# All projections of the second layer ahead of its attention: block products over 1024 tokens, results through DRAM

## The chip, the cores and the metric

The kernel runs on one core of one Trainium2 chip. TensorE (PE in the profile) multiplies matrices: it holds a 128x128 stationary operand and streams a moving operand of up to 512 columns past it into a bank of PSUM. VectorE (DVE), ScalarE (ACT) and GpSimd (POOL) do element-wise work; SyncE (SP) issues every DMA here, on one queue. The metric is device time of one execution in microseconds (us), as the median of several runs. Beside it there is one profiled execution with its own time and its span (first to last instruction).

## What is computed

A decoder trunk of two layers over 1024 tokens with model width 1024, all in 32-bit floating point.

```python
# layer 0: retention, 4 heads (query and key width 256, value width 512)
u = rms_norm(h, ret_norm_pre); q, k, v, g = split(u @ ret_w_in)
o = retention_chunkwise(rope(q), rope(k) / 16, v)
o = head_norm(o) * silu(g)
h = h + rms_norm(o @ ret_w_out, ret_norm_post)
# shared keys and values
k, v = split(rms_norm(h, kv_norm) @ w_kv)            # 8 heads: 128 and 256 wide
# layer 1: stick-breaking attention, 8 heads
q, g = split(rms_norm(h, sb_norm_pre) @ sb_w_in)
z = q @ k.T / sqrt(128)                              # strictly causal, s < t
A[t, s] = sigmoid(z[t, s]) * prod_{s < j < t} (1 - sigmoid(z[t, j]))
h = h + rms_norm((A @ v) * silu(g) @ sb_w_out, sb_norm_post)
```

Two norms act on the same residual stream after layer 0 (for keys and values, and for queries and gates), so both share one row of reciprocal root mean squares and differ only in their gains.

## The kernel before

**Numbers.** Every operand of a large product is split into a rounded high part and a remainder (`split`, lines 574 to 581: one ScalarE copy, one VectorE subtraction). A product is then three matmuls: high by high, high by low, low by high (`mm3`, lines 412 to 417). So a line of the profile that says L415, L416 or L417 is one of these three; the tile names tell which product it belongs to.

**Tiles.** The residual stream is held transposed, features on the partitions. The tokens go in two halves of 512. `xh` are the eight split tiles of a half's normalised stream, `whl` split weight tiles, `wraw` weights as loaded. PSUM has eight banks under four names: `ma`, `mb`, `z` and `o`, two each.

**Phases.** `run` (line 1521) walks through four phases: layer 0 for the first and second half ("A"), layer 1 for the first and second half ("C"). In a "C" phase there are four pairs of heads (`CPair`, line 1149). For each pair and half:

- `kqproj` (line 1155): keys and queries, features on the partitions, by `proj` (line 457): 8 k-tiles x 4 column blocks x 3 matmuls of 512 columns. The gain of the norm is multiplied into the weights when they are split (`gkq`, line 1142).
- `values` (line 1169): values with tokens on the partitions. Two pairs together form a matrix of 2 x 2 blocks (input features even and odd, token blocks of 256, 512 output columns each), multiplied with seven block products instead of eight (numbers 1 to 7). `vfirst` does five of the products with one pair, `vsecond` two with the next. The sums of the stream are written to DRAM (`T_d`, line 1098) and read again (`operand`, line 1219); the sums of weights for the second use too (`w_sums`, line 1107, to `S_d`).
- `gproj` (line 1305): gates by `proj` again, then the SiLU.
- `rows` (line 1319): for each head and block of 128 query tokens the scores (PSUM `z`), two sigmoids on ScalarE (lines 1337, 1338), the causal selection on GpSimd (lines 1342, 1343), a running product on VectorE (line 1345) and the product that gives the weights A (line 1346). The second half also meets the first half's keys, from DRAM (`k_d`).
- `mix` (line 1356): A is transposed on TensorE (line 1375), split to `AT`, and multiplied by the values into two `o` banks. `gate` (line 1396) multiplies by the gates and splits the result to `oT`.
- `out` (line 1316, `outproj` line 484): the output projection of a pair: its weights are loaded and split, the sum over the pairs is read from and written to DRAM for every block of 128 features (`y_d`). `finish` (line 1433) does the last pair in two half-width passes with the closing norm.

**Order.** `merge` (line 524) lays the steps of one piece beside those of another, for example a pair's scores beside its value products. The instructions written so are then put in order by a list scheduler, `arrange` (line 101): it knows each instruction's dependences, the number of buffers of every tile name (`BUFS`, line 319) and an estimated duration (`_time`, line 68), ranks instructions by how late they may run, and fixes one order for every engine's queue and for SP's. At run time each queue goes strictly in that order.

**Where the change sits.** The last output projection of layer 0's second half writes `y_d`; `a_post` (line 1008) reads it back, applies the closing norm, adds the input, writes the stream to `h_d`, and sums squares for the next norm. `c_prep` (line 1068) loads the stream of a half, multiplies it by the row and splits it.

Of the kernel before, what the change touches and what calls it, by code (L numbers as in the profile page):

```python
# [13 lines left out]
F32 = mybir.dt.float32  # L14
# [294 lines left out]
def trunk(ctx, tc, xT, wts, gains, trig, ident_in, cols, out):  # L309
# [174 lines left out]
    def outproj(base, oT, y_d, first, acc=None, tags=None):  # L484
# [4 lines left out]
        def sum_so_far(c):  # L489
            y = S("f2", [512])  # L490
            if not first:
                dma(y[:], y_d[c])
            return y
        sums = ahead(8, sum_so_far)

        def chunk(j):
# [21 lines left out]
            dma(y_d[c], y[:])  # L518
# [64 lines left out]
    def flat(x):  # L583
# [6 lines left out]
    k_d = [DRAM(f"k{h}", F32R) for h in range(8)]  # L590
    v_d = [[DRAM(f"v{p}{b}", F32R) for b in range(4)] for p in range(NPAIR)]
    T_d = [{n: [DRAM(f"T{t}{n}{i}", F32R) for i in range(2)] for n in (5, 6, 7, 4)} for t in range(2)]
    S_d = [{n: [dr.tile([128, 512], F32, tag=f"s{g}{n}{k}", name=f"s{g}{n}{k}") for k in range(4)]
            for n in (5, 6, 7, 3)} for g in range(2)]
# [131 lines left out]
    class AHead:  # L726
# [139 lines left out]
        def out(self, y_d, acc=None, tags=None):  # L866
            return outproj(self.base + 12, lambda: self.oT, y_d, self.h == 0, acc, tags)
# [140 lines left out]
    def a_post(t, y_d, acc):  # L1008
# [13 lines left out]
        def load(k):  # L1022
            y, raw = box[k] = pair(k) if t else (S("vo", [512]), S("vo", [512]))
            dma(y[:], y_d[k])
            dma(raw[:], xT[128 * k:128 * k + 128, HT * t:HT * t + HT])
# [36 lines left out]
    def pair(k):  # L1062

        x = S("S", [2, 512])
        return x[:, 0], x[:, 1]


    def c_prep(t):
        X = Ctx()
        X.xh = [None] * 8  # L1070
        raws = []

        def load(k):
            c2, c = divmod(k, 2)
            if c == 0:
                raw = S("S" if c2 < 2 else "A", [2, 512])
                raws.append(raw)
                dma(flat(raw), h_d[t][c2][:])
                V.tensor_tensor(raw[:], raw[:], rowh[0][:].unsqueeze(1).broadcast_to([128, 2, 512]), ALU.mult)
            x = X.xh[k] = hl("xh")  # L1080
            split((x[:, 0, :], x[:, 1, :]), raws[c2][:, c])

        def sums(kt):

            raw = raws[kt]
            for c in range(2):
                A_.activation(raw[:, c], raw[:, c], AF.Copy, scale=gcol(G_KV, 2 * kt + c))
            q = [raw[:, n // 2, 256 * (n % 2):256 * (n % 2) + 256] for n in range(4)]
            a, b = S("f2", [2, 256]), S("f2", [2, 256])
            V.tensor_tensor(a[:, 0], q[0], q[1], ALU.subtract)  # L1090
            V.tensor_tensor(a[:, 1], q[2], a[:, 0], ALU.subtract)
            V.tensor_tensor(b[:, 0], q[2], q[0], ALU.subtract)
            V.tensor_tensor(b[:, 1], q[3], a[:, 1], ALU.subtract)
            for f, ns in ((a, (5, 6)), (b, (7, 4))):
                x = S("AT", [2, 2, 256], F32R)
                split((x[:, :, 0, :], x[:, :, 1, :]), f[:])
                for j, n in enumerate(ns):
                    dma(T_d[t][n][kt // 2][:, 512 * (kt % 2):512 * (kt % 2) + 512], x[:, j].rearrange("p a b -> p (a b)"))

        X.sums = [lambda kt=kt: sums(kt) for kt in range(4)]  # L1100
        return X, [lambda k=k: load(k) for k in range(8)]

    def block(base, which, blk, kt):

        return wts[base + 4 + 16 * which + kt, :, 512 * blk:512 * blk + 512]

    def w_sums(g):

        base, box = 64 + 32 * g, {}

        def load(kt):
            if kt % 2:
                x = S("sc0", [2, 512])
                r = box[kt] = [x[:, 0], x[:, 1], S("tab", [512])[:], S("tab", [512])[:]]
            else:
                x, y = S("S", [2, 512]), S("S", [2, 512])
                r = box[kt] = [x[:, 0], x[:, 1], y[:, 0], y[:, 1]]
            for x, (which, blk) in zip(r, ((1, 0), (1, 1), (0, 0), (0, 1))):
                dma(x, block(base, which, blk, kt))

        def add(kt):
            b12, b22, b11, b21 = box[kt]
            V.tensor_tensor(b12, b12, b22, ALU.add)
            V.tensor_tensor(b11, b12, b11, ALU.subtract)
            V.tensor_tensor(b22, b22, b11, ALU.subtract)
            V.tensor_tensor(b21, b21, b11, ALU.subtract)
            for n, x in ((5, b12), (6, b11), (7, b22), (3, b21)):
                dma(S_d[g][n][kt][:], x)

        return in_turn(4, 1, load, add)  # L1130
# [11 lines left out]
    def gkq(kk):  # L1142
        return [(512 * c + 256 * s, 512 * c + 256 * s + 256, gcol((G_KV, G_SB)[s], 2 * kk + c))
                for c in range(2) for s in range(2)]

    def gone(which):
        return lambda kk: [(512 * c, 512 * c + 512, gcol(which, 2 * kk + c)) for c in range(2)]

    class CPair:
        def __init__(self, t, pr, X):  # L1150
# [535 lines left out]
```

## Time and profile before

| | |
|---|---|
| median of 3 runs | 1709.36 us (1708.68 to 1711.95) |
| profiled execution, its own time | 1709.47 us |
| its span | 1707.8 us |
| mean granted TensorE clock | 0.998 |
| matmuls | 8057 |
| busy: TensorE, VectorE, ScalarE, GpSimd | 1694.7, 1309.3, 888.2, 141.9 us |
| moved by DMA | 344.58 MB, 202 GB/s over the span |
| HBM read, written | 271.68 MB, 71.30 MB |

A group's row gives line, engine, operation, output tile, input tiles, shapes and count, then busy time and mean duration of one, then the idle time of that engine just before. TensorE's matmuls overlap one another, so their mean duration is more than the distance between two starts. The granted clock is a share of full speed.

### The profile page before, as it was taken

The numbers are of one execution on the slowest core, as the hardware profiler recorded it, in microseconds if no ns is written. First come the engines' busy times: TensorE is split into PE (matmuls) and PEld (weight loads), VectorE is DVE, ScalarE is ACT, GpSimd is POOL, SyncE is SP. The second block draws the span as 40 slices with busy tenths as digits, with TensorE's granted clock in tenths as the row PEclk, the third lists the DMA queues.
The fourth block names the chain that finished last, engine by engine and source line by source line (L and its number), as shares of the span: only waits on it lengthen the run. The fifth ranks groups of instructions, "written<-read, shape, count | busy, mean of one in ns | idle before, by whom it ended". The sixth has DMA issues, their size and how long they took to land.

```text
span 1707.8 us, 23993 instructions
## 1 busy us (share of the span) xinstructions
PE 1694.7 (99%) x8057; PEld 1414.8 (83%) x8057; DVE 1309.3 (77%) x2213; ACT 888.2 (52%) x1656; POOL 141.9 (8%) x275
## 2 busy tenths in 40 slices
PE   9999999999999999999999999999999999999997
PEld 7888888888888888888888888888888888888887
DVE  8766778799867988698878878667887756756865
ACT  6445546465545536355755544544665445545543
POOL 0000101010010000112010100000010001001001
PEclk9999999999999999999999999999999999999999
DMA  5226565667536676286886989667883763463523
GB/s 191 95 92 204 161 234 169 210 190 259 166 118 194 213 231 216 78 289 206 290 305 215 338 313 305 202 213 258 285 275 117 258 223 99 162 215 99 163 93 126
DMA packets 182250, 344.58 MB, mean 202 GB/s; under 512 B 20208, under 2 KB 24432, under 8 KB 182128
## 3 DMA queue, kind: packets, MB, share of 16 engines
q1 hardware_dynamic: 182128, 343.07, 60.9%
q8 instruction: 63, 1.03, 0.3%
q14 instruction: 59, 0.48, 0.1%
HBM read 271.68 MB, written 71.30 MB: 201 GB/s over the span
## 4 chain that ended last, share of the span: by engine, by line
PE 96%; DVE 2%; DMA 1%; issue 0%; ACT 0%; SPq 0%; POOL 0%; DVEq 0%
PE pmb L415 13%; PE pmb L417 12%; PE pmb L416 12%; PE pma L415 12%; PE pma L416 12%; PE pma L417 12%; PE po L417 5%; PE po L416 5%; PE po L415 5%; PE pz L1375 2%; PE pz L417 1%; PE pz L416 1%; PE pz L415 1%; PE pz L1003 1%; DMA ko<-in_xT_dram 0%; PE pz L551 0%
## 5 line engine op out<-in xcount | busy, mean ns | idle before, releaser
L577 ACT ACTIVATE whl<-wraw 128x512 fp32r<-128x512 f32 x322 | 190.3, 624 | 171.4 <-PE pmb L417 83.5
L578 DVE TENSOR_TENSOR whl<-wraw,whl 128x512 fp32r<-128x512 f32 x322 | 213.6, 686 | 65.8 <-ACT whl L577 64.8
L415 PE MATMUL pma<-xh,whl 128*128 128x512 f32 x384 | 153.1, 399 | 0.0
L415 PE MATMUL pmb<-xh,whl 128*128 128x512 f32 x384 | 152.5, 398 | 0.0
L417 PE MATMUL pma<-xh,whl 128*128 128x512 f32 x384 | 150.1, 391 | 0.0
L417 PE MATMUL pmb<-xh,whl 128*128 128x512 f32 x384 | 150.0, 391 | 0.0
L416 PE MATMUL pma<-xh,whl 128*128 128x512 f32 x384 | 149.9, 390 | 0.0
L416 PE MATMUL pmb<-xh,whl 128*128 128x512 f32 x384 | 149.7, 390 | 0.0
L580 ACT ACTIVATE whl<-wraw,gn 128x256 fp32r<-128x256 f32 (+1 forms) x146 | 82.0, 603 | 55.2 <-PE pmb L417 35.4
L1345 DVE TENSOR_TENSOR_SCAN sgn<-sgn 128x384 f32<-128x384 f32 (+4 forms) x64 | 86.6, 1355 | 28.0 <-POOL sgn L1343 27.9
L577 ACT ACTIVATE AT<-pz 128x512 fp32r<-128x512 f32 (+1 forms) x96 | 46.2, 486 | 108.3 <-PE pz L1375 106.3
L415 PE MATMUL pmb<-oT,whl 128*128 128x512 f32 x256 | 101.3, 396 | 0.0
L416 PE MATMUL pmb<-oT,whl 128*128 128x512 f32 x256 | 100.1, 391 | 0.0
L417 PE MATMUL pmb<-oT,whl 128*128 128x512 f32 x256 | 100.1, 391 | 0.0
L578 DVE TENSOR_TENSOR AT<-pz,AT 128x512 fp32r<-128x512 f32 (+1 forms) x96 | 52.9, 554 | 58.4 <-ACT AT L577 57.7
L1342 POOL TENSOR_SCALAR_AFFINE_SELECT A<-A 128x128 f32<-128x128 f32 x64 | 32.8, 513 | 770.5 <-ACT A L1337 770.5
L581 DVE SCALAR_TENSOR_TENSOR whl<-wraw,gn,whl 128x256 fp32r<-128x256 f32 (+1 forms) x146 | 83.8, 602 | 14.1 <-ACT whl L580 13.3
L577 ACT ACTIVATE whl<-S 128x512 fp32r<-128x512 f32 x104 | 63.4, 628 | 51.4 <-PE pmb L417 12.6
L417 PEld LDWEIGHTS pmb<-xh,whl 128*128 128x128 f32 x384 | 72.1, 188 | 15.8
L417 PEld LDWEIGHTS pma<-xh,whl 128*128 128x128 f32 x384 | 72.1, 188 | 15.6
L416 PEld LDWEIGHTS pmb<-xh,whl 128*128 128x128 f32 x384 | 72.3, 188 | 13.4
L415 PEld LDWEIGHTS pmb<-xh,whl 128*128 128x128 f32 x384 | 72.2, 188 | 13.4
(394 smaller groups left out, 4593.2 us busy)
## 6 DMA issues: line engine op xcount, KB each, us to landing
wraw<-in_wts_dram SPq DMA_DIRECT2D x521, 256.0 KB, 3.6
y<-f SPq DMA_DIRECT2D x120, 256.0 KB, 3.6
f<-y SPq DMA_DIRECT2D x88, 256.0 KB, 4.4
S<-in_wts_dram SPq DMA_DIRECT2D x44, 256.0 KB, 4.8
ko<-in_wts_dram SPq DMA_DIRECT2D x42, 256.0 KB, 4.6
vo<-in_wts_dram SPq DMA_DIRECT2D x41, 256.0 KB, 4.4
T<-AT SPq DMA_DIRECT2D x32, 256.0 KB, 4.8
sc<-T SPq DMA_DIRECT2D x16, 512.0 KB, 5.3
```

The source lines that it names most:

```text
L415: MM(p, lh, rh, start=start, stop=False, **kw)
L416: MM(p, lh, rl, start=False, stop=False, **kw)
L417: MM(p, ll, rh, start=False, stop=stop, **kw)
L577: A_.activation(dst[0], src, AF.Copy)
L578: V.tensor_tensor(dst[1], src, f32(dst[0]), ALU.subtract)
L580: A_.activation(dst[0], src, AF.Copy, scale=scale)
L581: V.scalar_tensor_tensor(dst[1], src, scale, f32(dst[0]), ALU.mult, ALU.subtract)
L1003: nc.tensor.transpose(pt[:, 128 * e:128 * e + 128], on[:, 128 * e:128 * e + 128], ident[:])
L1342: first = G.affine_select(a[:, dg], a[:, dg], [[-1, 128]], ALU.is_gt, 0.0, base=0, channel_multiplier=1)
L1345: V.tensor_tensor_scan(n[:, :W][:, ::-1], n[:, :W][:, ::-1], n[:, :W][:, ::-1], 1.0, ALU.mult, ALU.bypass)
L1375: nc.tensor.transpose(p[:, 128 * tb:128 * tb + 128], self.A[hh][tb][:, c0:c0 + 128], ident[:])
```

## The change

Layer 1 is written in a new order. All its projections, for all 1024 tokens, come first; their results go to DRAM; then sixteen heads (eight of each half) run one after the other, with the output projections beside them.

- **Keys, queries, gates** (`Feature`): the stream is a matrix of 2 x 2 blocks (features even and odd; first and second token half), and so are the weights of a pair (two column blocks of 256). Seven block products of 4 k-tiles, 2 output blocks of 128 and 512 tokens each take the place of the eight implicit in `proj`. Gains are multiplied into the loaded weights on ScalarE, sums of weights are made on VectorE, and the banks of PSUM go on accumulating from one product to the next where the scheme allows it.
- **Values** (`Values`): the seven products with blocks of 512 tokens, once for each group of two pairs.
- **The sums of the stream** are made once, in `w_turn`, between the two halves' streams, and stay in SBUF. Products 1 and 2 need the first half alone. Of three key and query pairs and one value group these two are computed before the turn ("early": product 1 goes to DRAM, `c_d`, and comes back later).
- **Output weights** are split once (`w_out`) beside the projections and stored split; `Att.out` loads them so. The running sum of the output projection stays in SBUF (`ys`).
- **Layer 0's last output projection** keeps its result in SBUF (`kept`), and `a_post` takes it from there.
- **The host** lays the weights of keys, queries and gates out by blocks (`_quads`).
- `T_d`, `S_d`, `c_prep`, `w_sums`, `CPair` and the rings of raw tiles go.

```diff
-    def outproj(base, oT, y_d, first, acc=None, tags=None):
+    def outproj(base, oT, y_d, first, acc=None, tags=None, kept=None):
...
-            dma(y_d[c], y[:])
+            if kept is None:
+                dma(y_d[c], y[:])
...
+    def w_turn(kept):
+        tags = {6: ["sgn", "sgn", "A", "ko"], 7: ["AT", "AT", "AT", "ko"], 4: ["v"] * 4}
+        B.x1, B.T = [None] * 4, {n: [None] * 4 for n in (5, 6, 7, 4)}
+        def make(kt):
+            q = [B.raws[kt][:, 0], kept[kt][:, 0], B.raws[kt][:, 1], kept[kt][:, 1]]
...
+            V.tensor_tensor(kept[kt][:], kept[kt][:], rowh[0][:].unsqueeze(1).broadcast_to([128, 2, 512]), ALU.mult)
+            B.x1[kt] = B.late[:, kt]
+            V.tensor_tensor(q[0], q[1], q[0], ALU.subtract)
+            V.tensor_tensor(q[1], q[3], q[1], ALU.subtract)
+            split((B.x1[kt][:, 0, :], B.x1[kt][:, 1, :]), q[3])
+            V.tensor_tensor(q[3], q[3], q[0], ALU.subtract)
+            V.tensor_tensor(q[2], q[2], q[3], ALU.subtract)
+            for n, r in ((5, q[0]), (6, q[3]), (7, q[1]), (4, q[2])):
+                x = B.T[n][kt] = B.far[:, kt] if n == 5 else hl(tags[n][kt])
+                split((x[:, 0, :], x[:, 1, :]), r)
...
+    class Feature:
...
+        def block(self, c, col):
...
+                    dma(raw, wts[self.base + 2 * c + col, :, 512 * i:512 * i + 512])
+                    for k in range(2):
+                        x = raw[:, 256 * k:256 * k + 256]
+                        A_.activation(x, x, AF.Copy, scale=gcol(self.gains[col], 2 * (2 * i + k) + c))
...
+        def chunk(self, n, e):
+            early, late = self.when == "early", self.when == "late"
+            over = {7: 6, 4: 6} if early else {6: 1, 7: 1, 4: 1}
...
+            p, w = self.bank[over.get(n, n)][e], self.w[n]
+            for kt in range(4):
+                x = B.x0[2 * kt + n - 1] if n < 3 else B.x1[kt] if n == 3 else B.T[n][kt]
+                at = slice(256 * kt + 128 * e, 256 * kt + 128 * e + 128)
+                mm3(p[:], w[:, 0, at], w[:, 1, at], x[:, 0, :], x[:, 1, :], fresh and kt == 0, kt == 3, goes_on=not fresh)
...
+    def put_kq(pr):
+        def put(t, col, e, src):
+            x = stage()
+            split((x[:, 0, :], x[:, 1, :]), src[:], QSCALE if col else None)
+            dma(kq_d[t][pr][2 * col + e][:], x[:, :, :].rearrange("p a b -> p (a b)"))
...
+    class Values:
...
+                for tb in tbs:
+                    tl = slice(128 * tb, 128 * tb + 128)
+                    mm3(banks[tb][:], x[:, 0, tl], x[:, 1, tl], w[:, 0, cl], w[:, 1, cl], fresh and kt == 0, kt == 3, goes_on=not fresh)
...
+    def w_out():
+        def one(pr, ng, i):
+            raw, x = raw_w(), stage()
+            dma(raw, wts[64 + 16 * pr + 12 + ng, :, 512 * i:512 * i + 512])
+            split((x[:, 0, :], x[:, 1, :]), raw)
+            dma(w_d[pr][ng][i][:], x[:, :, :].rearrange("p a b -> p (a b)"))
...
+    class Att:
...
+            tag = "xh" if hh else "A"
...
+                    for n in ("K", "Q"):
+                        box[n] = hl("xh")
+                        dma(flat(box[n]), kq_d[self.t][self.pr][hh + (2 if n == "Q" else 0)][:])
...
+                    g = S("sg", [512])
+                    dma(g[:], g_d[self.t][self.pr][j][:])
...
+        kq = [Feature(64 + 16 * p, (G_KV, G_SB), put_kq(p), "early" if p < 3 else "", c_d[p]) for p in range(NPAIR)]
...
+        full = (1, 2, 5, 6, 7, 3, 4)
+        order = [(x, n) for x in kq[:3] + [vs[0]] for n in (1, 2)]
+        opening = len(order)
+        order += [(x, n) for x in [vs[0]] + kq[:3] for n in (5, 6, 7, 3, 4)]
+        order += [(x, n) for x in kq[3:] + [vs[1]] + gs[:2] for n in full]
+        order += [(x, n) for x in gs[2:] for n in (1, 5, 6, 7, 4)]
+        ends = len(order)
+        order += [(x, n) for n in (2, 3) for x in gs[2:]]
...
+        for n in range(2, 16):
...
+            merge(A.mix(n % 2), (outs[8 * (n % 2):][:8], 0 if n % 2 else 1, 1), (rows_of(n + 1), 0, 1), (extra, 1, 1))
```

More of the change, by code (lines that the diff above doesn't have):

```diff
@@ L1100, in c_prep @@
[L1100 to L1130, printed above, removed]
+            x = B.x0[k] = hl("xh")
@@ L1420, in load @@
             c2, c = divmod(k, 2)
-            y, raw = box[k] = pair(k)
+            y, raw = box[k] = S("wraw", [512]), S("wraw", [512])
             dma(y[:], y_d[k])
@@ L1606, in run @@
[L1606 to L1616 removed]
+            else:
+                load = w_prep()
@@ L1618, in trunk @@
+        merge(first)
+        merge(second, (tail(0), 1, 1))
+        for s in tail(1):
+            s()
     run()
```

677 lines of the change are left out of this document (375 added, 302 removed).

## The prediction

> **What bounds the kernel now.** I read the page's busy times and chain of waits first, then the list of what TensorE waited for in the second layer, then stretches of that layer, then its groups and a few instructions in order of time. Columns of a stretch: its bounds and length, then busy time (count) of PE, PEld, DVE, ACT and POOL, the granted clock, the share of the DMA engines, GB/s.
>
> ```profile
> PE 1694.7 (99%) x8057; PEld 1414.8 (83%) x8057; DVE 1309.3 (77%) x2213; ACT 888.2 (52%) x1656; POOL 141.9 (8%) x275
> ...
> PE 96%; DVE 2%; DMA 1%; issue 0%; ACT 0%; SPq 0%; POOL 0%; DVEq 0%
> ```
>
> ```profile
> core 0 of [0], span 1707.8 us
> engine line waited for: us in total, times, longest us
> PE pz L1490 <- POOL col L1484: 1.0, 1, 1.0
> PE pz L1474 <- DVE acc L1467: 0.3, 1, 0.3
> PE pma L416 <- DVE qk L578: 0.2, 1, 0.2
> ```
>
> TensorE makes 96% of the chain. From 800 us on, where the second layer begins, it waited 1.5 us for others, 1.3 of that in the closing steps. So time is the sum of TensorE's steps, as long as the others keep up. How near they come:
>
> ```profile
> 750.00:775.00 25.00, 25.00 (x115) 20.71 (x114) 23.97 (x40) 17.00 (x32) 3.39 (x2) 1.00 0.86 281
> ...
> 950.00:1000.00 50.00, 50.00 (x241) 41.91 (x240) 35.71 (x62) 24.73 (x53) 6.97 (x13) 1.00 0.96 323
> ...
> sum 908.00, PE 898.20 PEld 754.41 DVE 668.44 ACT 470.92 POOL 70.14; mean PE 49.90 PEld 41.91 DVE 37.14 ACT 26.16 POOL 3.90
> ```
>
> VectorE was busy 23.97 of 25 us (96%) and DMA ran at 323 GB/s with TensorE still full. Neither is a bound until it passes those levels.
>
> **What is removed: matmuls.** A projection matmul streams 512 columns. The start-to-start step comes from a run of them without gaps (28 rows, first and last shown), the count from the groups between 800 us and the end:
>
> ```profile
> 1204.80 0.39 PE L416 MATMUL pmb<-qk,whl 128*128 128x512 f32 x1
> ...
> 1210.92 0.39 PE L416 MATMUL pma<-qk,whl 128*128 128x512 f32 x1
> ```
>
> ```profile
> L415 PE MATMUL pma<-xh,whl 128*128 128x512 f32 x256 | 102.3, 400 | 0.0
> L415 PE MATMUL pmb<-xh,whl 128*128 128x512 f32 x256 | 101.5, 397 | 0.0
> ...
> L415 PE MATMUL pmb<-qk,whl 128*128 128x512 f32 x32 | 12.4, 389 | 0.0
> ```
>
> (1210.92 - 1204.80)/27 = 0.2267 us a step; the 400 ns of the groups is a matmul's whole passage, of which the next hides nearly half. Keys, queries and gates are 2 x 256 x 3 = 1536 matmuls (three for each product of split numbers), as the loops say: 2 halves x 4 pairs x 2 kinds x 96. After the change, a pair and kind over 1024 tokens is 7 products x 2 column blocks x 4 k-tiles x 3 = 168 in place of 192, so 8 x 168 = 1344. The values have seven products already: 672 before and after. Scores, transposes, weighted sums and output projection keep their counts. So 192 steps go: 192 x 0.2267 = **43.5 us**. Against the profiled execution's 1709.47 us (span 1707.8, with 1.67 us around it; 0.11 above the median of the runs, 1709.36) that gives 1665.9 if nothing else changes.
>
> The Trainium skill (TensorE: Matmul & The Clock Gate, "Wait — 56ns, not 53.3ns?") has 215.7 ns as the warm step at 512 columns. By it 41.4 us would go and the sum would be 2.1 us higher. The row is 11 ns longer than the rule, and the sum goes by the row.
>
> **What is added before the attention.** The products for differences of the two token halves need the second half's normalised stream; only products 1 and 2 of three key/query pairs and of one value group can run before it: 3 x 2 x 24 + 2 x 48 = 240 matmuls, 54.4 us. In that time the first layer's closing norm must finish (eight adds with squares, two diagonals), and the turn forms all sums. VectorE's prices, from its groups between 760 and 1100 us (a 512-wide operation on two tiles is 0.69, with a scale 0.745):
>
> ```profile
> L581 DVE SCALAR_TENSOR_TENSOR whl<-wraw,gn,whl 128x512 fp32r<-128x512 f32 x21 | 15.6, 745 | 1.3 <-ACT whl L580 0.9
> L578 DVE TENSOR_TENSOR whl<-wraw,whl 128x512 fp32r<-128x512 f32 x23 | 15.4, 691 | 2.8 <-ACT whl L577 2.7
> ...
> L1030 DVE SCALAR_TENSOR_TENSOR S<-S,gn,acc 128x512 f32<-128x512 f32 x8 | 6.0, 748 | 6.5 <-ACT acc L571 3.6 <-DMA S<-y 2.9
> ...
> L1079 DVE TENSOR_TENSOR S<-S,acc 128x1024 f32<-128x1024 f32 x4 | 4.8, 1210 | 0.0
> ```
>
> - The norm: 8 scaled products 0.748, 8 sums and 7 squares' sums 0.69: 16.3; two diagonals of 8 narrow parts, each put at half of 0.69: 5.5.
> - The turn, four times: one 1024-wide product 1.21, four subtractions and five splits at 0.69: 4 x 7.4 = 29.7.
> - The three pairs' products 1 and 2: 12 weight splits, 6 sums, 6 output splits at 0.69: 16.6.
> - The value group, all seven products: 28 weight splits (16 scaled, 12 not), 16 scaled sums, 12 sums and 16 output splits: 32 x 0.745 + 40 x 0.69 = 51.4.
>
> Together 119 us of VectorE work for the 480 matmuls (108.8 us) up to the end of that value group. Some 6 us of it can lie outside (the first weights before, the last output splits after): 113 us. At 100% busy that is 4 us more than TensorE's work, at the best 96% shown 9 us. VectorE's queue is in order: weight splits and sums stand behind the turn, and TensorE waits for them. Bounds: below 0 to 12 us (more can be put off into the slack that follows; a gain below nothing is excluded, since no matmul disappears with a wait). I take **6**, nearest the two sums. After it an early pair's last five products take 120 x 0.2267 = 27.2 us against 34 VectorE operations, 23.5 us (10 weight splits, 8 weight sums, 10 output sums, 6 output splits); the 32 output-weight splits laid over about 220 us add 10%. That is about 96%: hidden, barely. A later pair or gate (36 operations, 24.8 us, in 38.1 us) has room. ScalarE gets 16 to 24 gain scalings a pair, at most 0.59 each (the 512-wide row below); with 14 weight splits, 8 output splits and 6 copies that is under 31 of 38 us: hidden.
>
> Stores and loads (keys, queries, values, gates and split output weights go to DRAM) are no engine's work but SP's and the DMA engines'; a value group reads and writes 8.4 MB each in 76.2 us, 220 GB/s, below the 323 shown.
>
> **What is moved: attention without projections beside it.** TensorE's 898.2 us from 800 us on, less 2208 x 0.2267 = 500.5 for projections, 21.8 for the first layer's last output projection (96 matmuls that fall there: half of the 2 x 32 x 3 of the third row above) and some 23 for the closing half-width projections (192 of 256 columns at 0.12, the step below), is 353 us, 22 us a head over sixteen. A head of the second token half has 36 matmuls of 512 columns and 16 transposes (128 columns) more:
>
> ```profile
> 1405.45 0.28 PE L416 MATMUL po<-AT,v 128*128 128x256 f32 x1
> 1405.57 0.28 PE L417 MATMUL po<-AT,v 128*128 128x256 f32 x1
> ...
> 1407.49 0.28 PE L416 MATMUL po<-AT,v 128*128 128x128 f32 x1
> 1407.60 0.27 PE L417 MATMUL po<-AT,v 128*128 128x128 f32 x1
> ```
>
> 36 x 0.2267 + 16 x 0.11 = 9.9 us more, so about 17 us a head in the first half and 27 in the second. What VectorE does there now, all scans and then all products of weights:
>
> ```profile
> 800.00:1708.00 908.00, 86.57 (x64) 1.00 0.65 217
> ```
>
> ```profile
> 800.00:1708.00 908.00, 47.57 (x64) 1.00 0.65 217
> ```
>
> By columns the second half has 3328 of every 4608, 72%: 7.8 and 4.3 us a head. With the splits of eight transposed blocks (4.7: four of full width 0.69, four shorter), gates 4 x 0.69 and output sums 4 x 0.69 it is 22.3 of 27 us, 83%, under the 96% once carried. So VectorE is covered by TensorE's output matmuls and the next head's scores; without that cover the chain of one row would show (second rival). Bounds for small waits: below 0 to 16 us (1 us a head). I take **2**, near the 0.2 us that stands for this kind of wait in the quoted list.
>
> Each head's loads also move past each other on SP's one queue: keys, queries, values, weights and gates, some 10 to 15 a head.
>
> ```profile
> L360 SPq DMA_DIRECT2D S<-h x12: 319/423/1086, 761.9 to 1345.5; - x12
> ```
>
> At the median 0.42 us that is 4 to 6 us of 17 to 27: hidden. The sum: 1709.47 - 43.5 + 6 + 2 = **1674 us**.
>
> **Rivals.**
> - *VectorE stays the bound past the turn.* 5 us more at each of the three early pairs: 1674 + 15 = 1689. For it: 96% demand; against: 96% was carried once.
> - *Attention hangs on its own chain (slower).* Each head's first transposed block needs its last row: three matmuls 0.68, two sigmoids 1.18, two selects 1.03, and by columns from the rows above (64 rows of 576 columns on average) scan 2.4 and product 1.3: 6.6 us; in the first half, half as wide, 4.7.
>
> ```profile
> L1342 POOL TENSOR_SCALAR_AFFINE_SELECT A<-A 128x128 f32<-128x128 f32 x64 | 32.8, 513 | 770.5 <-ACT A L1337 770.5
> ...
> L1337 ACT ACTIVATE A<-pz 128x512 f32<-128x512 f32 x48 | 28.0, 592 | 22.1 <-PE pz L417 21.6
> ```
>
> All uncovered: 8 x 6.6 + 8 x 4.7 = 90, so 1764. It decides from 40% uncovered (35.5 of 90). Against it: the next head's rows are laid beside this head's output matmuls (10.9 us).
> - *Loads bound the first eight heads.* Each loads 4.72 MB (weights 2.10, keys and queries 1.05, values 1.05, gates 0.52) in 17 us, 278 GB/s. At the second layer's mean of 217 (the rows of scans) it would take 21.8: 8 x 4.7 = 37 more, 1711, no change. The stretch at 323 speaks against it.
> - *The clock falls in one long gap at the turn.* The clock went to half within a few microseconds of the last matmul (before 1700 us):
>
> ```profile
> 1696.00:1700.00 4.00, 2.20 (x15) 1.67 (x13) 1.26 (x5) 1.45 (x4) 0.71 (x1) 0.99 0.35 122
> 1700.00:1704.00 4.00, 0.00 (x0) 0.00 (x0) 3.40 (x6) 0.00 (x0) 2.50 (x2) 0.50 0.24 83
> ```
>
> If the 6 us came in one piece, some 15 matmuls after it would take twice 0.2267: 3.4 more, and about as much in a second gap: 1681. The Trainium skill (TensorE: Matmul & The Clock Gate, "What's actually happening") states half rate after an idle window of about 3.4 us; the rows agree.
> - *The change does not save matmuls:* excluded by the loop counts.
>
> **How the numbers follow.** Forecast (1666 to 1684) 0.68; VectorE past the turn 0.15; clock 0.05; loads 0.04; attention chain 0.06; 0.02 for other times below before. The range 1664 to 1692 holds the forecast, the clock and most of VectorE's case, and reaches under 1665.9 only by the measurement's spread; it leaves out loads and the chain. About 0.2% (3.4 us) is what a measurement here tells from no change: faster 0.90, same 0.04 (loads), slower 0.06 (chain).
>
> **What would show it.** TensorE should have 7865 matmuls. The list of what TensorE waited for should show a few microseconds for VectorE's splits about 50 to 110 us after the first layer's end, VectorE near 95% there, and next to nothing between the heads. Wrong if TensorE waits for transposed blocks (chain) or for loads of keys, values or weights (DMA), or if its clock drops at the turn.

## The result and the profile after

The changed kernel takes 1671.97 us (median of 4 runs, 1671.11 to 1673.91) against 1709.93 us (4 runs, 1708.68 to 1711.95) for the kernel before: a ratio of 0.9778, 95% interval 0.9762 to 0.9795. It is faster by 38 us. The forecast was 1674, in a range of 1664 to 1692. The profiled execution of the changed kernel took 1673.91 us, 35.6 less than the one before (1709.47); the working below goes by these two.

The page's busy times and the engines' shares of the chain of waits, of the changed kernel:

```profile
PE 1653.1 (99%) x7865; PEld 1379.4 (82%) x7865; DVE 1290.6 (77%) x2127; ACT 881.1 (53%) x1660; POOL 128.6 (8%) x275
...
PE 95%; DVE 2%; DMA 2%; issue 0%; ACT 0%; SPq 0%; POOL 0%; DVEq 0%; ACTq 0%
```

TensorE has 7865 matmuls where it had 8057, the 192 fewer of the prediction, and its busy time is 41.6 us less. It still makes up 95% of the chain. What it lost in the second layer lies in a few places. First, the list of TensorE's waits in the changed kernel from 800 us to the end:

```profile
PE po L417 <- DVE oT L584: 2.1, 2, 1.3
PE pz L1010 <- DVE sgn L1006: 1.4, 1, 1.4
PE pz L1563 <- POOL col L1557: 1.0, 1, 1.0
PE pma L415 <- ACT qk L583: 0.9, 1, 0.9
PE pma L415 <- DVE sc L587: 0.6, 1, 0.6
PE pz L1547 <- DVE acc L1540: 0.4, 1, 0.4
PE pz L415 <- DVE f L1130: 0.3, 1, 0.3
PE pma L416 <- DVE qk L584: 0.2, 1, 0.2
```

Then stretches of it (bounds and length; busy time and count of PE, PEld, DVE, ACT, POOL; granted clock; DMA share; GB/s):

```profile
775.00:800.00 25.00, 23.63 (x112) 19.19 (x111) 20.29 (x35) 14.64 (x27) 8.60 (x14) 1.00 0.57 188
800.00:825.00 25.00, 23.93 (x100) 19.23 (x100) 19.51 (x31) 16.76 (x36) 0.00 (x0) 0.93 0.42 142
801.00:803.00 2.00, 1.47 (x3) 0.95 (x4) 2.00 (x4) 2.00 (x6) 0.00 (x0) 0.64 0.76 211
803.00:805.00 2.00, 2.00 (x6) 1.51 (x6) 2.00 (x4) 1.07 (x3) 0.00 (x0) 0.50 1.02 383
875.00:900.00 25.00, 22.40 (x94) 17.02 (x93) 25.00 (x39) 14.77 (x25) 0.00 (x0) 1.00 0.21 80
900.00:925.00 25.00, 25.00 (x112) 20.65 (x111) 24.96 (x42) 14.48 (x26) 0.00 (x0) 1.00 0.51 168
1070.00:1640.00 570.00, 569.84 (x2841) 480.64 (x2840) 405.96 (x591) 282.33 (x588) 45.37 (x129) 1.00 0.72 250
```

The rows at L1563 and L1547 are the closing steps, 1.4 us against 1.3 before. The others:

- **The turn** (875 to 900 us): TensorE idle 25.00 - 22.40 = 2.6 us. The list puts 2.1 of it down to the low halves of the fifth product's operand (`oT`) and 0.3 to a PSUM bank that VectorE still had to read (`f`). VectorE was busy all of 875 to 900 and 24.96 of the next 25 us.
- **The attention** (1070 to 1640 us): 0.16 us idle in 570.
- **The seam between the layers** (around 800 us), which the prediction had no term for: 1.37 + 1.07 = 2.44 us idle, and a clock of 0.93 over 25 us, which is 1.75 us of matmuls done late. The clock was at half from 801.6 to 805.0 us.

The kernel before had the same seam, with much less in it (stretches of the kernel before):

```profile
775.00:800.00 25.00, 24.31 (x115) 19.69 (x114) 20.70 (x39) 12.57 (x22) 7.75 (x13) 1.00 0.53 169
800.00:825.00 25.00, 25.00 (x111) 20.68 (x112) 22.47 (x41) 14.33 (x29) 0.00 (x0) 1.00 0.79 259
```

It lost 0.69 us there at full clock. So the budget is -43.5 (matmuls) + 2.6 (turn) + 0.6 (the wait for `sc`, just before the attention) + 0.2 (attention) + 1.75 (idle at the seam, 2.44 - 0.69) + 1.75 (its clock) = -36.6, against -35.6 measured. Of the 1.0 left, 0.6 is more idle time in the first 30 us (TensorE busy 27.28 us against 27.84), long before the change; all of it is within the 2.8 us by which four runs of this kernel differ.

### The profile page after: what moved, and what is told of

Its sections match the earlier page's. It is cut to its first block, busy times and chain, and to the rows that moved or that the text cites. A ratio compares the mean times of both kernels' runs of the same rounds, so it can differ in the third digit from the quotient of the medians.

```text
span 1672.2 us, 23341 instructions
## 1 busy us (share of the span) xinstructions
PE 1653.1 (99%) x7865; PEld 1379.4 (82%) x7865; DVE 1290.6 (77%) x2127; ACT 881.1 (53%) x1660; POOL 128.6 (8%) x275
## 2 busy tenths in 40 slices
DMA packets 170792, 359.23 MB, mean 215 GB/s; under 512 B 18224, under 2 KB 20400, under 8 KB 170672
## 4 chain that ended last, share of the span: by engine, by line
PE 95%; DVE 2%; DMA 2%; issue 0%; ACT 0%; SPq 0%; POOL 0%; DVEq 0%; ACTq 0%
PE pma L415 12%; PE pma L416 12%; PE pma L417 12%; PE pmb L415 10%; PE pmb L416 10%; PE pmb L417 10%; PE po L417 6%; PE po L416 6%; PE po L415 6%; PE pz L417 2%; PE pz L416 2%; PE pz L415 2%; PE pz L1452 2%; PE pz L1010 1%; PE pz L557 0%
## 5 line engine op out<-in xcount | busy, mean ns | idle before, releaser
L583 ACT ACTIVATE whl<-wraw 128x512 fp32r<-128x512 f32 x330 | 195.4, 624 | 187.1 <-PE pmb L417 82.8
L584 DVE TENSOR_TENSOR whl<-wraw,whl 128x512 fp32r<-128x512 f32 x330 | 218.9, 686 | 82.4 <-ACT whl L583 81.4
L1424 DVE TENSOR_TENSOR_SCAN sgn<-sgn 128x128 f32<-128x128 f32 (+3 forms) x64 | 86.6, 1353 | 18.0 <-POOL sgn L1422 18.0
L415 PE MATMUL pmb<-oT,whl 128*128 128x512 f32 x224 | 88.9, 397 | 0.0
L416 PE MATMUL pmb<-oT,whl 128*128 128x512 f32 x224 | 88.0, 393 | 0.0
L417 PE MATMUL pmb<-oT,whl 128*128 128x512 f32 x224 | 87.5, 391 | 0.0
L583 ACT ACTIVATE AT<-pz 128x512 fp32r<-128x512 f32 (+1 forms) x96 | 45.0, 491 | 71.8 <-PE pz L1452 70.8
L415 PE MATMUL pma<-xh,whl 128*128 128x512 f32 x200 | 78.9, 396 | 0.0
L416 PE MATMUL pma<-xh,whl 128*128 128x512 f32 x200 | 78.0, 390 | 0.0
L417 PE MATMUL pma<-xh,whl 128*128 128x512 f32 x200 | 78.0, 390 | 0.0
L583 ACT ACTIVATE whl<-S 128x512 fp32r<-128x512 f32 x92 | 56.0, 628 | 40.7 <-DVE S L804 8.7
L584 DVE TENSOR_TENSOR whl<-S,whl 128x512 fp32r<-128x512 f32 x92 | 62.1, 690 | 9.9 <-ACT whl L583 9.8
L415 PE MATMUL pmb<-xh,whl 128*128 128x512 f32 x160 | 63.7, 398 | 0.0
L415 PE MATMUL pma<-oT,whl 128*128 128x512 f32 x160 | 63.1, 397 | 0.0
L417 PE MATMUL pma<-oT,whl 128*128 128x512 f32 x160 | 62.9, 393 | 0.0
L416 PE MATMUL pma<-oT,whl 128*128 128x512 f32 x160 | 62.9, 393 | 0.0
L416 PE MATMUL pmb<-xh,whl 128*128 128x512 f32 x160 | 62.3, 389 | 0.0
L417 PE MATMUL pmb<-xh,whl 128*128 128x512 f32 x160 | 62.3, 390 | 0.0
L415 PE MATMUL pmb<-qk,whl 128*128 128x512 f32 x136 | 53.5, 394 | 0.0
L416 PE MATMUL pmb<-qk,whl 128*128 128x512 f32 x136 | 53.2, 391 | 0.0
L417 PE MATMUL pmb<-qk,whl 128*128 128x512 f32 x136 | 53.1, 391 | 0.0
```

What stands on the lines that cost most here:

```text
L415: MM(p, lh, rh, start=start, stop=False, **kw)
L416: MM(p, lh, rl, start=False, stop=False, **kw)
L417: MM(p, ll, rh, start=False, stop=stop, **kw)
L583: A_.activation(dst[0], src, AF.Copy)
L584: V.tensor_tensor(dst[1], src, f32(dst[0]), ALU.subtract)
L1424: V.tensor_tensor_scan(n[:, :W][:, ::-1], n[:, :W][:, ::-1], n[:, :W][:, ::-1], 1.0, ALU.mult, ALU.bypass)
```

## The experiments

In all that follows "the changed kernel" is 1671.97 us; the kernel before was measured again beside each group of runs (1709.7 to 1710.2), and every ratio is to that.

### Does the number of matmuls set the time?

The first product of each of the eight key/query and gate features is done twice: 8 x 24 = 192 matmuls more, nothing else.

```diff
-            for kt in range(4):
+            for turn in range(2 if n == 1 else 1):
+                for kt in range(4):
```

> The changed kernel with product 1 of each of the eight key/query and gate features computed twice, the first pass thrown away by the second's fresh start: 8 x 24 = 192 matmuls of 512 columns more, so the matmul count of the kernel before, and nothing else added. Theory (the gain is the matmuls removed, at 0.2267 us a step): 1672.0 + 43.5 = 1715.5 us, or up to 2.6 us less, since three of the eight extra passes lie ahead of the turn and give VectorE time. Rival (the gain came from less work of VectorE and fewer rounds through DRAM, with TensorE only following): well under half of that, below 1692 us.

1716.85 us (1714.68 to 1718.44), ratio 1.0042 [1.0028, 1.0055]. That is 44.9 us over the changed kernel, and 192 x 0.2267 is 43.5: matmuls cost what the prediction gave them, and with all 8057 of them the new order alone is 7 us slower than the kernel before. Fewer rounds through DRAM cannot be the gain either: DMA moved 359.23 MB in the changed kernel and 344.58 MB in the one before. The extra matmuls ahead of the turn did not shorten its waits (2.2 us for `oT` again): the steps of the second norm stand in TensorE's queue behind them, so the row arrived 16 us later as well.

### How much of the turn depends on the work before it?

Four early features in place of three, then two (`p < 2`); the lists that set the order of the pieces follow.

```diff
-        kq = [Feature(64 + 16 * p, (G_KV, G_SB), put_kq(p), "early" if p < 3 else "", c_d[p]) for p in range(NPAIR)]
+        kq = [Feature(64 + 16 * p, (G_KV, G_SB), put_kq(p), "early" if p < 4 else "", c_d[p]) for p in range(NPAIR)]
...
```

> Products 1 and 2 of all four key/query pairs ahead of the turn instead of three: 48 more matmuls, 10.9 us, before the first product that needs the second half's stream; VectorE gets 4 sums and some gain scalings are added on ScalarE. Theory (the wait at the turn comes from a burst that starts when the row of the second norm arrives, too late for the first products that need it): the 2.6 us of waits between 885 and 893 us vanish, 1669.4 us. Rival (VectorE's total work up to the end of the first value group is the bound, as the prediction had it): VectorE's work falls by less than TensorE's, a gain of at most 1 us, 1671 to 1673.

> Products 1 and 2 of only two key/query pairs ahead of the turn: 48 matmuls, 10.9 us, and 5.5 us of VectorE's work less before it. Theory (burst after a late row): TensorE waits about 10.9 us more at the turn, 1683 us. Rival (total work of VectorE): the difference 10.9 - 5.5 = 5.4 more, 1677 us; if the turn does not bind at all, 1672.

With four: 1669.54 us (1668.59 to 1670.98), ratio 0.9768 [0.9754, 0.9781]; the turn's waits fell to 1.5 us, all for the sixth product's operand now. The time is the one that the theory gave, but not by its sum: the turn gained 1.1 us in place of 2.6, and the seam between the layers, too, cost less here (1.8 us idle at full clock). With two: 1682.38 us (1679.88 to 1685.39), ratio 0.9842 [0.9828, 0.9855]. TensorE's waits and two stretches of the kernel with two early features:

```profile
PE po L415 <- ACT oT L583: 2.7, 1, 2.7
PE po L417 <- DVE oT L584: 2.2, 1, 2.2
PE pma L415 <- ACT A L583: 2.2, 1, 2.2
```

```profile
875.00:900.00 25.00, 19.36 (x66) 14.40 (x67) 24.26 (x40) 12.72 (x23) 0.00 (x0) 0.82 0.24 85
900.00:925.00 25.00, 25.00 (x109) 20.62 (x108) 22.93 (x38) 15.87 (x30) 0.00 (x0) 0.97 0.67 215
```

Some 8 us of waits, and a clock of 0.82 and 0.97 that costs 4.5 + 0.75 = 5.2 us more. The waits are 5.6 us more than in the changed kernel, which is the rival's 5.4 (total work of VectorE) and not the 10.9 of the theory; the time came near the theory's 1683 because the clock added its 5.2. This is the prediction's clock rival, seen with a shorter cover. The cover of early products is what the turn lives on.

### Is it the order of VectorE's queue at the turn, or the lateness of the row?

First, the turn in two passes: in all four quarters the fifth product's operand before anything for the other products.

```diff
-            split((B.x1[kt][:, 0, :], B.x1[kt][:, 1, :]), q[3])
...
+            x = B.T[5][kt] = B.far[:, kt]
+            last = split((x[:, 0, :], x[:, 1, :]), q[0])
+            B.rest.append((kt, q))
+            if kt < 3:
+                return
+            for kt, q in B.rest:
...
+                turns.extend((last.ins.name, z.ins.name) for z in firsts)
```

> The turn's work unchanged in amount, but all of VectorE's work for the stream of product 5 (four products with the row, four subtractions, four splits) is put ahead of the rest of the turn. Theory (burst in the wrong order: twelve other pieces of 0.60 us stood between the splits of product 5): the waits between 885 and 893 us shrink by 2 us or more, 1669 to 1670. Rival (total work of VectorE): the same 2.6 us only come a product later, 1672.

1677.1 us (1676.58 to 1679.33), ratio 0.9812 [0.9799, 0.9826]: slower. The waits for `oT` went, and others came (TensorE's waits in this kernel):

```profile
PE pma L417 <- DVE A L584: 2.0, 1, 2.0
PE pma L417 <- DVE sgn L584: 0.6, 1, 0.6
```

They are for the sixth product's operand, and the clock fell to 0.93 from 900 to 925 us. Putting one product first only moved the lack of VectorE's time to the next. The seam, too, came out worse here (3.2 us idle, clock 0.86), since the list scheduler laid it out anew. Then the row of the second norm asked for earlier:

```diff
-        for j, k in zip((1, 2, 3, 3, 4, 5, 6, 8, 9, 10, 11, 13, 14, 15), range(len(post))):
+        for j, k in zip((1, 2, 3, 3, 4, 5, 6, 7, 8, 9, 10, 11, 12, 13), range(len(post))):
```

> The closing norm's last steps (sums, squares, statistics, row) are written two places, about 5.4 us, earlier among the opening products; the amount of work is the same. Theory (the row of the second norm arrives too late): the row comes some 5 us earlier, the 2.6 us of waits at the turn vanish, 1669.4. Rival (VectorE's total work up to the value group's end binds, as four early pairs and the fives first suggest by their remaining 1.5 and 3.1 us of waits): VectorE is near full from 850 to 925 us either way and the waits stay, 1671 to 1673.

1673.59 us (1673.31 to 1675.14), ratio 0.9792 [0.9777, 0.9807]. The row came 3.3 us earlier (871.0 us) and the turn still cost 2.4 us in the same kind of waits, 1.3 of them for `oT`. The low halves of the fifth product's operand in this kernel:

```profile
L584 DVE TENSOR_TENSOR oT<-A,oT x4: 682/684/686, 878.1 to 895.0; 128x512 fp32r<-128x512 f32 x4
```

The last came at 895.0 us, no earlier than in the changed kernel (894.5, shown below): weight sums and splits of the value group, which had stood ahead of the row in VectorE's queue, now stood behind it, and VectorE waited once for TensorE (1.05 us). Lateness of the row alone is not it.

### Is it the sum of VectorE's work?

Eight of VectorE's sixteen differences at the turn are left out. The splits and products stay and read what lies there, so these operands hold other numbers.

```diff
-            V.tensor_tensor(q[1], q[3], q[1], ALU.subtract)
             split((B.x1[kt][:, 0, :], B.x1[kt][:, 1, :]), q[3])
-            V.tensor_tensor(q[3], q[3], q[0], ALU.subtract)
```

> The changed kernel with eight of VectorE's sixteen differences at the turn left out (the two lines per quarter that make the operands of products 6 and 7 and stand between the first product's operand and its split); the splits and every product read what lies there instead, so the numbers computed are others, and all other instructions stay. These eight cost VectorE 8 x 0.60 = 4.8 us in 876 to 895 us of the changed kernel. Theory that VectorE's sum of work binds at the turn: TensorE's waits for the splits there fall from 2.4 us to 0.5 or less and the time by 1.5 to 2.5 us, to 1669.5 to 1670.5, the seam costing what it costs in the changed kernel. Rival, that a chain of single steps binds (row, scaling, first difference, copy, low half: each waits for the one before): the waits stay at 1.5 us or more and the time at 1671 to 1673.

1669.0 us (1665.94 to 1670.67), ratio 0.9761 [0.9747, 0.9775], 3.0 below the changed kernel. There were no waits between 840 and 975 us at all. In the changed kernel the row of the norm came at 874.26 us (start, duration, engine, line):

```profile
874.26 0.60 ACT L577 ACTIVATE acc<-pz 128x512 f32<-128x512 f32 x1 [1.33 <-PE pz L575]
```

and the low halves of the fifth product's four quarters, by tile (count, shortest, median and longest in ns, first and last start, then who waited for them, us and times):

```profile
L584 DVE TENSOR_TENSOR oT<-A,oT x4: 679/681/682, 880.8 to 894.5; 128x512 fp32r<-128x512 f32 x4
...
  PE po L417: 2.1, 2
```

The same rows without the eight differences, where nobody waited for them, and a stretch of that kernel:

```profile
870.83 0.60 ACT L577 ACTIVATE acc<-pz 128x512 f32<-128x512 f32 x1 [1.33 <-PE pz L575]
```

```profile
L584 DVE TENSOR_TENSOR oT<-A,oT x4: 682/684/685, 876.0 to 885.2; 128x512 fp32r<-128x512 f32 x4
```

```profile
875.00:900.00 25.00, 25.00 (x112) 20.64 (x111) 24.93 (x40) 15.19 (x29) 0.00 (x0) 1.00 0.17 64
```

From the row to the last quarter's low half it was 20.2 us (894.5 - 874.26) and is 14.4 now (885.2 - 870.83), 5.9 less, where the eight differences are 8 x 0.60 = 4.8 (the step of 0.60 is shown below). TensorE asks for the quarters one after another and no longer finds one missing. A chain of single steps (row, scaling, difference, copy, low half) would not have been shortened, since none of the eight differences lies in it. So the turn's waits come from the amount of work in VectorE's queue between the row and the fifth product, as the earlier row also says, which gained nothing while that amount grew. The 1.1 us beyond the 4.8 are other work that the list scheduler laid elsewhere. The time fell 0.4 us more than the 2.6 of the turn; this kernel's own runs lie 4.7 apart.

### What makes the seam?

The first guess was late weights, for want of a free buffer: take the first loads of the second layer from two other buffers.

```diff
-        ring[:] = ["wraw", "wraw", "wraw", "vo", "vo"]
+        ring[:] = ["vo", "vo", "wraw", "wraw", "wraw"]
```

> The second layer's first loaded weights (product 1 of the first pair) take buffers that nothing uses at the end of the first layer, in place of buffers of the weights' ring that come free late; nothing else. Theory (at the seam between the layers ScalarE's queue stood 1.88 us before the gain scaling of these weights, and the last head's normalisation behind it, so that TensorE idled 2.4 us in the profile between 798 and 803 us and ran some 3 us at a half-rate clock): most of these 4 us go, 1668 to 1670. Rival (the seam is set by the first layer's own chain, normalisation and transposes): unchanged, 1671 to 1673.

1674.37 us (1673.31 to 1675.38), ratio 0.9795 [0.978, 0.9809], the seam idle 2.7 us: not confirmed. The next was the order of ScalarE's queue. Rows of the changed kernel around 800 us, in order of time:

```profile
794.52 0.84 POOL L968 TENSOR_TENSOR small<-small,small 128x1 f32<-128x1 f32 x1
...
795.25 0.91 ACT L1149 ACTIVATE wraw<-wraw,gn 128x256 f32<-128x256 f32 x2 [1.88 <-DMA wraw<-in_wts_dram]
...
796.54 1.14 ACT L583 ACTIVATE xh<-A 128x512 fp32r<-128x512 f32 x2
...
797.79 0.51 ACT L1149 ACTIVATE wraw<-wraw,gn 128x256 f32<-128x256 f32 x1
...
798.08 0.39 PE L417 MATMUL pmb<-oT,whl 128*128 128x512 f32 x1
798.20 0.76 ACT L980 ACTIVATE sgn<-po,small,small 128x512 f32<-128x512 f32 x1
...
799.83 0.63 PE L1010 MATMUL pz<-ident,sgn 128*128 128x128 f32 x4 [1.37 <-DVE sgn L1006]
```

GpSimd had the last normalisation's factors ready at 795.4 us. ScalarE began that normalisation (L980) at 798.20, behind gain scalings of the second layer's weights (L1149), one of which had itself waited for its load, and behind copies that came after it (L583). TensorE had nothing left after 798.47. So the normalisation was put ahead of the first feature's gain scalings, in the changed kernel, then in the one with four early features, then in the one with four early features and the earlier row.

```diff
-                A_.activation(on, p[:], AF.Identity, scale=r[:], bias=nb[:])
+                last_norm[:] = [A_.activation(on, p[:], AF.Identity, scale=r[:], bias=nb[:])]
...
-                        A_.activation(x, x, AF.Copy, scale=gcol(self.gains[col], 2 * (2 * i + k) + c))
+                        z = A_.activation(x, x, AF.Copy, scale=gcol(self.gains[col], 2 * (2 * i + k) + c))
+                        if self.base == 64:
+                            turns.append((last_norm[0].ins.name, z.ins.name))
```

> The changed kernel with one thing different: ScalarE may scale no weight tile of the second layer's first key-and-query feature by its gains before it has written the first layer's last normalisation. Everything else, the number of instructions of each kind too, is as in the changed kernel. Theory: at the seam between the layers TensorE waits because this normalisation stands in ScalarE's queue behind gain scalings whose weights are still on their way (in the changed kernel it ran at 798.20 us although GpSimd was done with its inputs at 795.4). Then it runs within about 0.7 us of GpSimd's end, TensorE's idle time in 775 to 825 us falls from 2.4 us to under 1, the clock shows no drop there, and the time falls by 1.5 to 4 us, to 1668 to 1670.5. Rival A: the chain itself (statistics, GpSimd, normalisation, gating, transposes, split) is longer than the work that TensorE has left, and ScalarE's order is not what decides: idle 2 us or more as before, time 1671 to 1673. Rival B: the scalings that now come later make the first product's weights late, and the wait only moves to the first matmuls that read them: the idle time at the normalisation goes and as much comes after 805 us, time 1671 to 1675.

1671.19 us (1670.04 to 1673.35), ratio 0.9777 [0.9763, 0.979]. TensorE's waits at the seam and a stretch of this kernel:

```profile
PE pma L415 <- ACT qk L583: 0.9, 1, 0.9
PE pma L416 <- DVE qk L584: 0.3, 1, 0.3
PE pz L1010 <- DVE sgn L1006: 0.2, 1, 0.2
```

```profile
800.00:825.00 25.00, 24.56 (x107) 20.15 (x108) 20.98 (x34) 18.44 (x39) 0.00 (x0) 1.00 0.43 141
```

The normalisation in the kernel before:

```profile
795.90 0.77 ACT L973 ACTIVATE sgn<-po,small,small 128x512 f32<-128x512 f32 x1
```

and in this one:

```profile
796.45 0.77 ACT L980 ACTIVATE sgn<-po,small,small 128x512 f32<-128x512 f32 x1
```

It began 1.75 us earlier than in the changed kernel (798.20), the wait for the normalised tile fell from 1.4 to 0.2 us and the clock stayed at 1.00, so this order did make that wait. It still came 1.9 us after GpSimd's end (794.56 us), not within the 0.7 expected, since ScalarE did a copy of a transposed block first. The idle time from 775 to 825 us is 1.4 us, over the 1 expected. About 1.2 us stay: the copy and the low half of the last transposed block, with nothing else for TensorE to do. Between the profiled executions the gain is 3.0 us, but the medians differ by 0.8 with overlapping ranges, so its worth by itself is not settled: 1671.19 lies in the range of rival A.

> The same order of ScalarE's queue, in the variant with four early features in place of three (1669.5 us alone, where the seam cost 1.8 us of idle time and no lower clock, and the turn 1.5 us). Theory of the queue's order: the seam's idle time falls under 1 us and the time by 0.8 to 1.8 us, to 1667.7 to 1668.7. Rival (the chain is as long as before, or the wait moves to the weights): 1669 to 1671.

1669.98 us (1669.12 to 1672.23), ratio 0.9767 [0.9754, 0.9781], no gain over four early features alone. There the wait for the normalised tile was only 0.6; it went, and the two waits behind it grew to 1.3 and 0.5. The rival held.

Before the third, the four early features with the earlier row alone:

> Four early pairs and the norm's last steps two places earlier together. Four pairs alone had 1669.5 us with 1.5 us of waits at the turn. Theory (late row): these 1.5 us go too, 1668. Rival (total work): 1669 to 1670, and what four pairs alone gained came from the seam (1.8 us idle at full clock there in place of 2.4 us idle and 1.7 us lost to the clock), not from the turn.

1672.02 us (1670.51 to 1672.62), ratio 0.978 [0.9765, 0.9794]. The turn had no waits left, but the seam idled 3.2 us and its clock was 0.93, and that took the gain back. With the normalisation put first:

> Four early features, the second norm's row asked for earlier, and the same order of ScalarE's queue at the seam. The row and the four features alone took every wait out of the turn, but the time was 1672.0 us, with 3.2 us of idle time and a lower clock (0.93) at the seam. If the seam is what ate that gain: turn 0 to 0.5 us, seam under 1 us and clock 0.99 or more between 800 and 825 us, time 1666.5 to 1668.5, the fastest of all. If something else did: 1670 to 1672.5 although the seam's waits are shorter.

1667.82 us (1667.24 to 1669.51), ratio 0.9754 [0.9741, 0.9768]: the fastest of all, and 4.2 us below the changed kernel with no overlap of the runs. Stretches of this kernel:

```profile
800.00:825.00 25.00, 24.59 (x108) 20.13 (x108) 20.32 (x33) 19.13 (x41) 0.00 (x0) 1.00 0.41 129
875.00:900.00 25.00, 25.00 (x112) 20.72 (x111) 24.15 (x38) 15.43 (x28) 0.00 (x0) 1.00 0.36 116
```

No idle time at the turn, full clock at the seam; 2.0 us of idle time stay there, over the 1 us that was expected. Against the kernel without the new order (1672.02) it is 4.2 us, of which 1.3 us of idle time and 1.75 of clock are seen in the two profiles; whether the clock holds in every run of it is open, since the drop does not follow the idle time alone (last section).

### Is the attention's own chain covered?

Both heads of a pair get their weights A from one tile name, so the rows of the next head must wait for buffers of this one.

```diff
-            tag = "xh" if hh else "A"
+            tag = "A"
```

> Attention weights of both heads of a pair go to one set of five buffers instead of two sets in turn, so that a head's rows can hardly be computed before the head ahead of it has been transposed; no instruction is added or removed. Theory (the chain of a row, 4.7 to 6.6 us a head by the prediction, is hidden only since the next head's rows run one head ahead): TensorE waits 2 to 5 us a head, 28 to 70 us over fourteen heads, 1700 to 1742. Rival (the output projection's matmuls would cover the chain anyway): under 5 us, below 1677.

1676.04 us (1674.95 to 1678.86), ratio 0.9802 [0.9786, 0.9819]: 4 us, not the tens that the chain would cost bare. A stretch of this kernel over the attention:

```profile
1070.00:1640.00 570.00, 567.79 (x2810) 477.87 (x2809) 403.63 (x587) 281.69 (x585) 46.32 (x129) 1.00 0.72 250
```

TensorE idled 2.2 us in 570, so other work of TensorE still covers the chain when the rows are held back. They were: ScalarE waited 20.1 us, in seven places, for a transpose to free the buffer of its next row (`A`), where the changed kernel has no such wait.

## Why the prediction was right, point by point

- **"What is removed: matmuls", -43.5.** Held: 192 fewer in the profile, and 44.9 us for putting 192 back.
- **"What is added before the attention", +6 at the turn.** The mechanism was right (waits for VectorE's splits behind the turn, with VectorE full there), the size was too large: 2.6 us. Two parts of the term were off: the price of VectorE's operations, and the stretch over which they were summed. The prediction added up listed durations, 0.69 us for 512 columns and 0.745 with a scale. At the turn, where VectorE's queue is full, operations listed at 0.68 start every 0.60 us (VectorE's rows of the changed kernel in order of time):

```profile
880.78 0.68 DVE L584 TENSOR_TENSOR oT<-A,oT 128x512 fp32r<-128x512 f32 x1
881.38 0.68 DVE L1130 TENSOR_TENSOR f<-po,f 128x512 f32<-128x512 f32 x1
881.98 0.68 DVE L1107 TENSOR_TENSOR v<-v 128x512 f32<-128x512 f32 x1
882.58 0.68 DVE L1130 TENSOR_TENSOR f<-pz,f 128x512 f32<-128x512 f32 x1
```

Cut in that ratio, 0.60 to 0.68, the list's 119 us become about 105 and the 113 inside the stretch about 100, an estimate below TensorE's 108.8. In the trace these 480 matmuls lie between 825.1 and 941.0 us, and VectorE was busy 107.5 of those 115.9, some work that the list does not have included. So the sum over the whole stretch was no bound: most of VectorE's pauses lie ahead of the row (19.28 of 25 us busy from 825 to 850), where the turn's work could not begin. The prediction had the right place and the right cause, with a sum over too long a stretch. What binds is the shorter one from the row (874.3 us) to the fifth product's last quarter, 20.2 us of VectorE's work without a pause, as the kernel with eight operations fewer showed. The Trainium skill (VectorE: DVE Perf Modes, "The TRN2 errata") gives (N + 151)/0.96, 691 ns at 512 columns, as the duration of one such operation. The listed durations agree (0.68 us); the steps between starts are shorter here, and a sum of queued work goes by the steps.
- **"What is moved", +2 for small waits in the attention.** 0.16 us from 1070 to 1640, and 0.6 just before. The rival of the attention's own chain is out.
- **"VectorE stays the bound past the turn", 1689.** Did not come: from 900 to 925 us VectorE was full (24.96 of 25), from 925 to 1040 us, which hold the early pairs' last products, it was busy 97.39 of 115, and TensorE lost nothing in either.
- **"Loads bound the first eight heads", 1711.** Did not come; 0.16 us of idle time in 570 leaves no room for it.
- **"The clock falls in one long gap at the turn", 1681.** Not at the turn. The mechanism is real, though: it came at the seam in the changed kernel and at the turn with two early features. Its price was mis-sized: a single drop cost 1.7 us (last section), half of the 3.4 in the prediction.
- **What was missing.** The seam between the layers has no term in the prediction: 1.75 us more idle time and 1.75 of lower clock. The step that left it out is "Against the profiled execution's 1709.47 us ... that gives 1665.9 if nothing else changes": the last normalisation of the first layer began 2.3 us later than before (798.20 against 795.90), in a queue of ScalarE that now held gain scalings. The prediction counted these scalings only against ScalarE's total time (under 31 of 38 us), not against the place where they stand in its queue. With the normalisation ahead of them 1.1 of the 1.75 us of idle time went; what makes the rest is open, and so is whether the 1.75 us of clock hang on this order, since the clock also fell in a kernel where TensorE did not wait for this tile at all (first products done twice).

The forecast of 1674 came as near as it did because the terms that were too large (turn 3.4, attention 1.2) and the one that was missing (3.5) nearly cancel in the profiled execution. That is luck.

## What to carry to other kernels

When TensorE sets the time, count its instructions first; a new order then costs what it leaves uncovered, and that is to be looked for at every place where one phase's last chain meets the next phase's first loads, not only where the change was made. Price an engine's queued work by the distance between starts in a dense stretch, and sum it from the moment its input arrives to the moment its result is asked for, with all else that the queue holds between the two. Work added to an engine with much free time can still stand in front of a critical instruction in its queue.

## What the runs showed of the hardware

- **The clock drops for 3.4 us at a time, without one long gap, and not each time.** At the seam of the changed kernel TensorE was idle for 1.37 us, did four transposes and was idle for 0.87 us; the clock went to half at 801.6 us, during the matmul that followed, and was back at 805.0 (0.57 from 801.5 to 802.0, 0.50 to 804.5, 1.00 from 805.0). Between 775 and 950 us the fourteen profiles show nine drops: seven of 3.4 us and two of 6.8 (at the seam with the fifth product first, at the turn with two early features). So 3.4 us at half clock cost 1.7 us each time. Over the profiled executions the idle time at the seam does not sort the drops: 0.93 with 1.5 us (first products done twice) and 2.4 us (the changed kernel), full clock with 2.2 us (eight operations fewer) and 2.7 us (other buffers first). Nor was one long gap needed at the end of the kernel before, on which the prediction's clock rival rests: there the clock fell at 1699.9 us, 0.2 us after TensorE's last transposes, with one gap of 1.03 us before them. The Trainium skill (TensorE: Matmul & The Clock Gate, "What's actually happening") says that activity is judged in free-running windows of about 3.4 us, and that a kernel's slow start therefore varies from run to run. The lengths of the drops here fit such a window; that its phase decides whether a drop comes would fit too, and no run tests it.
- **VectorE's listed durations overlap.** 0.68 us listed, 0.60 from start to start, where no operation waits for anything.
